# Modulation weights loaded from the POOL queue instead of SP's, transfers of the compressed blocks from ScalarE's

## Chip, cores and metric

The kernel runs on one core of a Trainium2 chip. The metric is the device time of one execution in microseconds (us). The median of three runs of the kernel before is 2730.47 us (2729.22 to 2731.21).

## What is computed

Two transformer blocks run one after the other on one sequence of 256 tokens with 2048 channels, all in float32. The change touches only the start of the first block: the modulation (adaLN), which gives six vectors of 2048 channels from a 2048 x 12288 matrix, and the compressed blocks of one of the four token mixers.

```python
def first_block(x, c, ...):
    c_act = jax.nn.silu(c)
    mod = c_act @ ada_w[l] + ada_b[l]                    # 2048 x 12288
    sh1, sc1, g1, sh2, sc2, g2 = jnp.split(mod, 6, axis=-1)
    h = rmsnorm(x, norm1_g[l]) * (1.0 + sc1[:, None]) + sh1[:, None]
    x = x + g1[:, None] * token_mixer(h, w_in[l], ...)   # four attention mixers
    h = rmsnorm(x, norm2_g[l]) * (1.0 + sc2[:, None]) + sh2[:, None]
    x = x + g2[:, None] * moe_ffn(h, ...)                # 16 experts
    return rmsnorm(x, final_g)
# second_block: a Hyena mixer, whose long filters depend on the weights alone and are
# computed at the start of the kernel; a gating unit; a dense feed-forward layer
```

## The kernel before

The program is unrolled, and a scheduler of the language gives each engine a fixed order of instructions by priorities and estimated times. Float32 products are made of three products of split parts: each chunk of weights, 128 x 1024 values or 512 KB, is loaded (L178) into a ring of five buffers (tag "wraw"), ScalarE rounds it to its high part (L144), VectorE subtracts for the low part (L147), and TensorE multiplies (L156 to L158). There are three buffers for each part.

The first stage has two phases. `phase0` loads the sequence (xT, L491), computes the filters of the second block (`filters`, at low priority: its last layer at L532, with weights loaded at L494 and a decay loaded at L497, its transforms at L549 to L559), and then goes through four blocks of 512 channels. For each block, `ada_steps` computes shift and scale, `norm_mod` makes h of the block, and `feed` multiplies it with the first columns of w_in. The modulation of the next block runs along with the products of this one. `mixers` then computes the other products of w_in and the four attention mixers, and a hook places the rest of the modulation (four more vectors) between them.

Every modulation load is a piece of 256 rows x 512 columns, 512 KB; there are 192 of them, 64 in `phase0`, 16 for each block. They share four buffers (tag "a"). All are issued from SP's queue (L438), the one that loads the ring too, so that all loads of weights stand in one line. Half of the pieces behind `phase0` are multiplied on VectorE (L446, L448), all others on TensorE (L444). At the end of `phase0` the variable `last_ada` holds the last load, and the loads of the next product (columns from 4608) are tied behind it by `tc.issue_after`.

`cmp_blocks` copies keys and values within SBUF to a layout with two tokens on the partitions: eight transfers from POOL's queue (L881, L882), which wait for a copy of ScalarE (L602), and memsets on POOL. `compress` multiplies these blocks after the product with the columns from 4608. POOL has no other work but a few memsets. ScalarE's queue issues small loads, the store of the filters (L571) and the bias tables (L764).

Of the kernel before, what the change touches and what calls it, by code (L numbers as in the profile page):

```python
# [15 lines left out]
PSUM = bass.MemoryType.PSUM  # L16
DRAM = bass.MemoryType.DRAM

P = 128
S = 256  # L20
D = 2048
KD = D // P
# [10 lines left out]
def _constants():  # L33
    """Arrays that depend on the shapes alone."""
    c = {}
# [24 lines left out]
    # compressed blocks [2 x 15] to 16 rows a head, and the head of each row  # L60
# [6 lines left out]
    # The DFT of 512 points of real data: planes of cos at 0..127, cos at 128, 255..129, -sin at both; the sine of 0  # L67
    # makes room for the highest frequency
    turn = 2 * np.pi / 512
# [10 lines left out]
    # the same by even and odd points: cos and -sin at 0..127 for even, for odd, then both at 128  # L80
# [15 lines left out]
def host(inputs):  # L96
    """The arrays of the launch."""
    a = {n: np.asarray(t) for n, t in inputs.items()}
    given = {n: np.ascontiguousarray(a[n]) for n in _NAMES}
    given.update(_layout(a, _constants()))  # L100
    return given


def _rows(*parts):
    """Parts [rows <= 128, columns] side by side, on 128 rows."""
    return np.concatenate([np.pad(p, ((0, P - len(p)), (0, 0))) for p in parts], 1)


def _layout(a, c):
    """Small arrays side by side, vectors by channel, x with its channels first."""  # L110
# [4 lines left out]
    w = {}  # L115
# [16 lines left out]
# columns of p_vec behind the square matrices, by 128 channels  # L132
# [5 lines left out]
class Body:  # L138
# [14 lines left out]
    def mm3(self, ps, a, b, start, stop):  # L153
        """ps (+)= a.T @ b for pairs (hi, lo) of stationary a and moving b."""
# [14 lines left out]
    def rload(self, src, kt, n, tag=None):  # L169
        """The DMA of a chunk of weights into the ring, or into a piece."""  # L170
# [10 lines left out]
    def wload(self, src, kt, width, perm=False):  # L181
        """kt row tiles x width columns of a float32 matrix -> (hi, lo).

        perm: columns of heads 0..7 in the order 0 4 1 5 2 6 3 7."""
# [19 lines left out]
    def gemm(self, w, nk, col0, width, xs, pieces, hook=None, perm=False):  # L204
        """Products of the columns col0.. of w [nk*128, *] with the activations.

        pieces: ("C", c, n): channel-major [n<=128 columns from c, 256 tokens];
                ("T", c, n, tok): token-major [128 tokens of tile tok, n columns from c].
        xs(k): the (hi, lo) channel-major activations of row tile k.
        """  # L210
# [8 lines left out]
    def accumulators(self, pieces):  # L219
        """PSUM of the pieces of a gemm: a bank holds two channel-major ones."""  # L220
# [12 lines left out]
    def feed(self, ps, w, k0, n, nk, col0, width, xs, pieces, perm=False):  # L233
        """The n row tiles from k0 of a gemm."""
        src = w[k0 * P:(k0 + n) * P, col0:col0 + width].rearrange("(k p) n -> p k n", p=P)
        wh, wl = self.wload(src, n, width, perm)
        for ip, p in enumerate(pieces):
            for kk in range(n):
# [4 lines left out]
                if p[0] == "C":  # L243
                    # two accumulators of a bank: the first product of one opens both, the last of the other closes both
# [12 lines left out]
    def sq_acc(self, acc, src, k, scale=1.0):  # L257
        """acc (+)= (src * scale)**2."""
# [8 lines left out]
    def scaled_split(self, hh, hl, k, g):  # L267
        """(hi, lo) of xT * g for row tile k; the factors of the tokens follow behind the products."""
# [12 lines left out]
    def token_ms(self, *parts):  # L281
        """Mean squares + eps of each token, [128 tokens, 2], from parts of the sums of each partition."""
# [10 lines left out]
    def token_rsqrt(self, v, then=None):  # L293
        """v[:, 2:4] = 1/sqrt(v[:, 0:2]), with one Newton step. then: a function whose table to load behind the root."""
# [7 lines left out]
    def spread(self, r):  # L302
        """[128 tokens, 2] -> the same 256 values on every partition."""
# [16 lines left out]
    def run(self):  # L320
# [25 lines left out]
        # pieces of 1024 values a partition: modulation weights, keys and values, then weights and tokens of experts  # L346
# [17 lines left out]
    def phase0(self):  # L364
        nc, tc, i = self.nc, self.tc, self.i
        tc.cur_priority = 10000
        with ExitStack() as c0:
# [3 lines left out]
            # silu(c), one column per row tile, in 32 equal columns each  # L371
# [15 lines left out]
            # Shift and scale by blocks of 512 channels, h of each block, and its products with the first  # L387
            # columns of w_in
# [6 lines left out]
            # the modulation of a block runs along with the products of the block before it  # L395
# [19 lines left out]
    def norm_mod(self, hh, hl, k, rstd, g, sc, sh):  # L415
        """(hi, lo) of row tile k of h = xT * rstd * g * (1 + scale) + shift, channel-major."""
# [10 lines left out]
    def ada_steps(self, seg, b, dve=False):  # L427
        """512 channels of one of the six vectors, in 4 steps of four row tiles: on VectorE, or on TensorE, which
        takes the four at a time, on 32 columns each. The sums come together behind a turn of rows to columns."""
# [4 lines left out]
        for q in range(4):  # L434
            for h in range(2):
                k0 = 4 * q + 2 * h
                raw = self.piece([P, 2, 512], "a")
                self.last_ada = nc.sync.dma_start(raw, w[k0 * P:(k0 + 2) * P, c0:c0 + 512]  # L438
                                                  .rearrange("(k p) n -> p k n", p=P))
# [42 lines left out]
    def filters(self):  # L482
# [21 lines left out]
        # the last layer comes twice, on the two halves of the partitions  # L504
# [18 lines left out]
        for o in range(2):  # L523
            for hf in range(2):
# [27 lines left out]
                # a sum over the even points and one over the odd points give two frequencies  # L552
# [21 lines left out]
    def mixers(self):  # L574
# [9 lines left out]
        bg, last = rest(), self.last_ada  # L584
# [9 lines left out]
        with ExitStack() as c0:  # L594
# [21 lines left out]
            # D  # L616
# [7 lines left out]
            with tc.issue_after(last.ins):  # L624
# [971 lines left out]
```

## Time and profile before

| What | Value |
|---|---|
| Median of three runs | 2730.47 us |
| Span of the profiled execution | 2723.2 us |
| Mean granted clock of TensorE (share of full speed) | 0.988 |
| TensorE busy | 2625.9 us (96%) |
| VectorE, ScalarE busy | 1797.8 us (66%), 1335.5 us (49%) |
| POOL busy | 5.3 us, 18 instructions |
| DMA moved | 640.81 MB, mean 235 GB/s |

The profiled execution's own time is known by its span, from the first to the last instruction. The three runs were timed without a profile; their median is 7.3 us above that span, which is what lies around it. Busy times are those of instructions: matmuls are pipelined, and one that waits inside the pipeline counts as busy. PE is TensorE, PEld its loading of weights, DVE VectorE, ACT ScalarE; "SPq", "ACTq" and "POOL ... DMA_DIRECT2D" are transfers being issued. "L444" is line 444 of the kernel. "[2.39 <-ACT whi L144]" behind an instruction is the time that its engine stood idle before it, and what ended it.

### The profile page before, as it was taken

What the parts mean: (1) busy time and instruction counts of PE and PEld (TensorE: products, weight loads), DVE (VectorE), ACT (ScalarE), POOL (GpSimd) and SP (SyncE); (2) the same over time, 40 slices, a digit from 0 to 9 for tenths busy, and PEclk for the clock granted to TensorE, in tenths of its full rate; (3) what the DMA queues carried; (4) which work ended last, traced back from release to release, by engine and by line L of the source; (5) the groups of instructions that cost most, each with busy time, mean ns of one, the idle gap of its engine ahead of it and who ended that gap; (6) DMA issues with size and microseconds to landing.
All of it is one profiled execution on the core that took longest, in us unless ns stands there. A gap on an engine that the chain in (4) does not pass through costs nothing.

```text
span 2723.2 us, 43658 instructions
## 1 busy us (share of the span) xinstructions
PE 2625.9 (96%) x17355; PEld 2274.9 (84%) x17355; DVE 1797.8 (66%) x2509; ACT 1335.5 (49%) x1774; POOL 5.3 (0%) x18
## 2 busy tenths in 40 slices
PE   6999999998999999999999899999999999999997
PEld 2467888897778776776998899999999999998886
DVE  4547767777888887887777655555655555555444
ACT  2333444546777766676444444444544444443443
POOL 0000000000000000000000000000000000000000
PEclk8999999998999999999999999999999999999999
DMA  8898898983999999996654566666566666666664
GB/s 305 305 308 293 294 320 301 329 294 107 314 323 309 331 322 331 321 338 236 182 158 139 166 183 183 183 185 186 181 184 185 181 184 184 181 185 193 186 188 136
DMA packets 320083, 640.81 MB, mean 235 GB/s; under 512 B 21564, under 2 KB 35420, under 8 KB 319104
## 3 DMA queue, kind: packets, MB, share of 16 engines
q1 hardware_dynamic: 310768, 618.83, 69.7%
q10 hardware_dynamic: 8848, 18.61, 2.0%
q8 instruction: 137, 2.24, 0.3%
q0 software_dynamic: 256, 0.52, 0.1%
q14 instruction: 74, 0.61, 0.1%
HBM read 631.01 MB, written 6.35 MB: 234 GB/s over the span
## 4 chain that ended last, share of the span: by engine, by line
PE 59%; DMA 8%; DVE 5%; ACT 3%; issue 1%; ACTq 1%; DVEq 0%; SPq 0%
PE ps_mm L158 16%; PE ps_mm L157 16%; PE ps_mm L156 16%; DVE wlo L147 4%; DMA wraw<-in_exp_w_down_dram 3%; DMA wraw<-in_exp_w_up_dram 3%; ACT whi L144 2%; DMA wraw<-in_exp_w_gate_dram 1%; PE ps_y L157 1%; PE ps_u L157 1%; PE ps_y L158 1%; PE ps_y L156 1%; PE ps_u L158 1%; PE ps_u L156 1%; PE ps_g L157 1%
## 5 line engine op out<-in xcount | busy, mean ns | idle before, releaser
L147 DVE TENSOR_TENSOR wlo<-wraw,whi 128x1024 fp32r<-128x1024 f32 (+1 forms) x972 | 1165.8, 1205 | 712.2 <-ACT whi L144 701.2
L144 ACT ACTIVATE whi<-wraw 128x1024 fp32r<-128x1024 f32 (+1 forms) x972 | 1011.6, 1044 | 1029.9 <-PE ps_mm L157 550.0
L156 PE MATMUL ps_mm<-hH,whi 128*128 128x256 f32 x3216 | 917.6, 285 | 8.5 <-ACT whi L144 7.1
L158 PE MATMUL ps_mm<-hH,wlo 128*128 128x256 f32 x3216 | 913.9, 285 | 2.8 <-DVE wlo L147 2.8
L157 PE MATMUL ps_mm<-hL,whi 128*128 128x256 f32 x3216 | 912.8, 284 | 0.0
L156 PEld LDWEIGHTS ps_mm<-hH,whi 128*128 128x128 f32 x3216 | 616.3, 192 | 31.7 <-issue 13.8
L158 PEld LDWEIGHTS ps_mm<-hH,wlo 128*128 128x128 f32 x3216 | 615.3, 192 | 17.3 <-DVE wlo L147 8.2
L157 PEld LDWEIGHTS ps_mm<-hL,whi 128*128 128x128 f32 x3216 | 616.4, 192 | 5.0 <-issue 4.6
L157 PE MATMUL ps_mm<-wlo,actH 128*128 128x512 f32 x352 | 139.3, 396 | 0.0
L158 PE MATMUL ps_mm<-whi,actL 128*128 128x512 f32 x352 | 139.1, 395 | 0.0
L156 PE MATMUL ps_mm<-whi,actH 128*128 128x512 f32 x352 | 139.0, 395 | 0.0
L157 PE MATMUL ps_y<-wlo,piece 128*128 128x512 f32 x256 | 106.4, 416 | 8.4 <-DVE wlo L147 7.8
L444 PE MATMUL ps_ada<-piece,cact 128*32 128x512 f32 x512 | 102.2, 637 | 7.3 <-DMA piece<-in_ada_w_dram 6.6
L158 PE MATMUL ps_y<-whi,piece 128*128 128x512 f32 x256 | 101.3, 397 | 0.0
L156 PE MATMUL ps_y<-whi,piece 128*128 128x512 f32 x256 | 92.7, 403 | 2.1 <-ACT piece L144 1.4
L448 DVE SCALAR_TENSOR_TENSOR arow<-piece,cs,arow 128x512 f32<-128x512 f32 x120 | 89.4, 745 | 0.9
L157 PEld LDWEIGHTS ps_mm<-wlo,actH 128*128 128x128 f32 x352 | 66.0, 187 | 16.3 <-DVE wlo L147 0.2
L156 PEld LDWEIGHTS ps_mm<-whi,actH 128*128 128x128 f32 x352 | 66.0, 187 | 16.0
L158 PEld LDWEIGHTS ps_mm<-whi,actL 128*128 128x128 f32 x352 | 66.0, 187 | 15.9
L157 PEld LDWEIGHTS ps_y<-wlo,piece 128*128 128x128 f32 x256 | 48.4, 189 | 34.6 <-DVE wlo L147 24.0
L156 PE MATMUL ps_mm<-mgH,whi 128*128 128x256 f32 x256 | 71.9, 281 | 0.0
L157 PE MATMUL ps_mm<-mgL,whi 128*128 128x256 f32 x256 | 71.9, 281 | 0.0
(446 smaller groups left out, 3486.8 us busy)
## 6 DMA issues: line engine op xcount, KB each, us to landing
wraw<-in_w_in_dram SPq DMA_DIRECT2D x224, 512.0 KB, 4.6
piece<-in_ada_w_dram SPq DMA_DIRECT2D x192, 512.0 KB, 5.0
wraw<-in_w_ffn_in_dram SPq DMA_DIRECT2D x176, 512.0 KB, 4.5
wraw<-in_exp_w_down_dram SPq DMA_DIRECT2D x125, 512.0 KB, 5.8
wraw<-in_exp_w_up_dram SPq DMA_DIRECT2D x124, 512.0 KB, 5.0
wraw<-in_exp_w_gate_dram SPq DMA_DIRECT2D x122, 512.0 KB, 5.0
wraw<-in_w_ffn_out_dram SPq DMA_DIRECT2D x88, 512.0 KB, 3.7
wraw<-in_w_out_dram SPq DMA_DIRECT2D x64, 512.0 KB, 5.1
```

The costliest lines, as they stand in the source:

```text
L144: self.nc.scalar.activation(dst, src, AF.Copy)
L147: self.nc.vector.tensor_tensor(dst, src, h.bitcast(F32), OP.subtract)
L156: mm(ps, a[0], b[0], start=start, stop=False)
L157: mm(ps, a[0], b[1], start=False, stop=False)
L158: mm(ps, a[1], b[0], start=False, stop=stop)
L444: nc.tensor.matmul(ps[m:m + 32], self.cact[:, k], r, start=q == 0, stop=q == 3)
L448: nc.vector.scalar_tensor_tensor(sb, r, self.cs[:, k:k + 1], sb, OP.mult, OP.add)
```

## The change

All modulation pieces are loaded from POOL's queue. The eight transfers of the compressed blocks go from POOL's queue to ScalarE's, and the six memsets in `cmp_blocks` and `nsa` from POOL to VectorE, so that POOL's queue holds modulation loads alone. The tie of the loads for columns 4608 behind the last modulation load is taken out, as it held on SP's queue. The numbers of buffers, the sizes and the arithmetic stay the same. The rest of the diff takes out comments.

```diff
@@ ada_steps
                 raw = self.piece([P, 2, 512], "a")
-                self.last_ada = nc.sync.dma_start(raw, w[k0 * P:(k0 + 2) * P, c0:c0 + 512]
-                                                  .rearrange("(k p) n -> p k n", p=P))
+                nc.gpsimd.dma_start(raw, w[k0 * P:(k0 + 2) * P, c0:c0 + 512]
+                                    .rearrange("(k p) n -> p k n", p=P))
...
@@ mixers
-        bg, last = rest(), self.last_ada
+        bg = rest()
...
-            with tc.issue_after(last.ins):
-                for m, p in enumerate(self.gemm(w, KD, 4608, 512, xs, C4, hook)):
-                    take(kv[:, m], p)
+            for m, p in enumerate(self.gemm(w, KD, 4608, 512, xs, C4, hook)):
+                take(kv[:, m], p)
...
@@ cmp_blocks
-        nc.gpsimd.memset(kk[64:, :, 255:], 0.0)
+        nc.vector.memset(kk[64:, :, 255:], 0.0)
         for h in range(2):
-            nc.gpsimd.dma_start(kk[:64, h], src[h * 64:h * 64 + 64])
-            nc.gpsimd.dma_start(kk[64:, h, :255], src[h * 64:h * 64 + 64, 1:])
+            nc.scalar.dma_start(kk[:64, h], src[h * 64:h * 64 + 64])
+            nc.scalar.dma_start(kk[64:, h, :255], src[h * 64:h * 64 + 64, 1:])
         blk = mp.tile([P, 16, 2, 16], F32, name="blk", tag="s", bufs=3)
-        nc.gpsimd.memset(blk[:, :, :, 15:], 0.0)
+        nc.vector.memset(blk[:, :, :, 15:], 0.0)
...
@@ nsa
-            nc.gpsimd.memset(s, 0.0)
+            nc.vector.memset(s, 0.0)
```

## Rows read from the trace of the kernel before

**Rows 1.** The page: its first line and TensorE's busy time, and the modulation loads in its list of issues (count, KB of each, median us from issue to landing).
```profile
span 2723.2 us, 43658 instructions
PE 2625.9 (96%) x17355; PEld 2274.9 (84%) x17355; DVE 1797.8 (66%) x2509; ACT 1335.5 (49%) x1774; POOL 5.3 (0%) x18
...
piece<-in_ada_w_dram SPq DMA_DIRECT2D x192, 512.0 KB, 5.0
```

**Rows 2.** Busy time by stretch. Columns: the stretch, its length, busy us and instructions of PE, PEld, DVE, ACT and POOL, the granted clock of TensorE, DMA's share, GB/s.
```profile
0.00:53.30 53.30, 30.53 (x104) 7.01 (x104) 23.07 (x52) 12.19 (x16) 0.20 (x4) 0.87 0.86 294
53.30:162.00 108.70, 103.06 (x556) 51.31 (x556) 61.88 (x126) 32.69 (x58) 0.69 (x5) 1.00 0.88 308
162.00:176.00 14.00, 11.65 (x83) 11.34 (x83) 7.16 (x13) 7.54 (x16) 0.00 (x0) 0.88 1.05 394
176.00:565.00 389.00, 382.76 (x2882) 320.01 (x2881) 284.35 (x498) 178.55 (x360) 4.37 (x9) 0.99 0.89 303
```

**Rows 3.** The same view in slices of 4 and 2 us.
```profile
4.00:8.00 4.00, 1.11 (x2) 0.28 (x2) 1.04 (x3) 0.21 (x1) 0.00 (x0) 1.00 1.08 444
...
16.00:20.00 4.00, 3.84 (x16) 0.84 (x14) 4.00 (x1) 1.10 (x1) 0.00 (x0) 1.00 0.88 263
...
28.00:32.00 4.00, 3.21 (x8) 0.66 (x7) 1.24 (x2) 0.00 (x0) 0.00 (x0) 0.50 0.50 145
...
60.00:64.00 4.00, 2.04 (x11) 0.56 (x8) 3.96 (x8) 2.21 (x4) 0.00 (x0) 1.00 1.05 396
...
170.00:172.00 2.00, 2.00 (x19) 2.00 (x18) 1.23 (x1) 1.31 (x3) 0.00 (x0) 1.00 1.03 396
```

**Rows 4.** The timeline of SP's queue from the start: when a run of issues began, how long it took from the first to the last, line, tile and source, number of issues.
```profile
1.65 0.43 SPq L491 DMA_DIRECT2D xT<-in_p_x_dram  x1
2.13 42.19 SPq L438 DMA_DIRECT2D piece<-in_ada_w_dram  x20
44.36 0.46 SPq L178 DMA_DIRECT2D wraw<-in_w_in_dram  x1
44.88 1.26 SPq L494 DMA_DIRECT2D piece<-in_p_w_dram  x2
...
46.88 1.30 SPq L497 DMA_DIRECT2D piece<-in_k_decay_dram  x2
```

**Rows 5.** The timelines of ScalarE, VectorE and TensorE near the first products: start, duration, instruction, idle time before it.
```profile
26.39 0.42 ACT L518 ACTIVATE fh<-fa 128x256 f32<-128x256 f32 x1
...
43.95 0.69 DVE L459 COPY arow<-ps_ada 128x512 f32<-128x512 f32 x1 [9.30 <-PE ps_ada L444]
...
53.30 0.39 PE L156 MATMUL ps_mm<-hH,whi 128*128 128x256 f32 x1 [2.39 <-ACT whi L144]
...
53.97 1.13 PE L532 MATMUL ps_b<-piece,fh 64*128 64x512 f32 x2
```

**Rows 6.** TensorE's groups of instructions by line from 53.3 to 175 us, those of the filters: count, busy us, mean ns of one, idle time before.
```profile
L557 PE MATMUL ps_b<-piece,fdft 128*128 128x512 f32 x32 | 16.8, 623 | 0.2 <-DVE piece L540 0.2
L532 PE MATMUL ps_b<-piece,fh 64*128 64x512 f32 x32 | 13.3, 642 | 0.0
L549 PE MATMUL ps_b<-vec,piece 128*128 128x1 f32 x64 | 8.4, 253 | 1.7 <-DVE piece L545 1.7
L559 PE MATMUL ps_b<-piece,fdft 128*1 128x512 f32 x16 | 8.2, 591 | 0.0
```

**Rows 7.** SP's waits from 44 to 162 us (us in total, times, the longest); the modulation loads of 44 to 160 us (shortest, median and longest issue in ns, first and last start) and the landing of the pieces in that stretch; last, the landing in the stretch from 160 to 570 us.
```profile
SPq L438 <- PE ps_ada L444: 69.6, 31, 7.1
...
L438 SPq DMA_DIRECT2D piece<-in_ada_w_dram x45: 367/368/1016, 43.9 to 153.4; - x45
...
DMA to landing us min/median/max: 3.8/5.3/10.4
...
DMA to landing us min/median/max: 3.5/5.4/7.6
```

**Rows 8.** The timelines of TensorE and of SP's queue near 340 us: two bursts of products of pieces (four records for a piece) and the loads between them.
```profile
339.20 1.92 PE L444 MATMUL ps_ada<-piece,cact 128*32 128x512 f32 x16
348.58 2.20 PE L444 MATMUL ps_ada<-piece,cact 128*32 128x512 f32 x16
...
340.29 2.16 SPq L438 DMA_DIRECT2D piece<-in_ada_w_dram  x4
```

**Rows 9.** Transfers of POOL and of ScalarE: the first four of POOL's eight by tile, and the landing of all eight; ScalarE's store of the bias table (48 KB) by tile, and its landing; an instruction of VectorE that ran while POOL issued; VectorE's products of a piece with a scalar, by tile.
```profile
L881 POOL DMA_DIRECT2D kk<-piece x4: 523/523/656, 176.2 to 179.4; - x4
...
DMA to landing us min/median/max: 5.2/6.0/6.5
...
L479 ACTq DMA_DIRECT2D ebias_d<-ebias x1: 335/335/335, 29.5 to 29.5; - x1
DMA to landing us min/median/max: 1.6/1.6/1.6
...
177.12 2.36 DVE L147 TENSOR_TENSOR wlo<-wraw,whi 128x1024 fp32r<-128x1024 f32 x2 [5.20 <-ACT whi L144]
...
L446 DVE TENSOR_SCALAR arow<-piece,cs x8: 470/478/488, 206.7 to 550.8; 128x512 f32<-128x512 f32 x8
```

**Rows 10.** The timeline of ScalarE where the keys and values to be compressed are copied out.
```profile
175.48 0.66 ACT L602 ACTIVATE piece<-ps_mm 128x256 f32<-128x256 f32 x2 [2.22 <-PE ps_mm L158]
176.02 2.01 ACT L144 ACTIVATE whi<-wraw 128x1024 fp32r<-128x1024 f32 x2
```

## The prediction

> **What bounds the kernel now.** The change touches only the stage before the experts, so I read that stage first. The page says that TensorE is busy for 96% of a span of 2723.2 us [rows 1]; a share over the whole kernel does not say what one stage waits for, so the next view is the busy time by stretch [rows 2]. The reader should see four stretches. From 0 to 53.3 us TensorE is busy for 30.53 us only, at a mean clock of 0.87, while DMA moves 294 GB/s. From 53.3 to 162 us it is busy for 103.06 of 108.70 us. A short end of the phase follows, from 162 to 176 us, and then 176 to 565 us with 382.76 of 389.00 us busy. So behind 176 us there is almost no idle time to win (6.2 us); what can be won lies before it.
>
> Second, is DMA full? In slices of 2 and 4 us [rows 3] the engines move 390 to 444 GB/s when loads of several kinds are under way (4 to 8, 60 to 64, 170 to 172 us), and 263 and 145 GB/s when modulation pieces are the only loads (16 to 20, 28 to 32 us). The share column reads 0.88 at 263 GB/s, so it is no measure of fullness here: what limits is how many loads are in flight. The modulation has four slots (tag "a").
>
> Third, SP's order [rows 4]: behind xT come 20 modulation loads that take until 44.3 us to issue, since each waits for a slot; the first chunk of w_in (44.36), the filters' last layer (44.88) and the decay (46.88) stand behind them. The price is in rows 5: the filters' input is ready at 26.8 us, their first matmul of the last layer comes at 53.97, and the first product of w_in at 53.30, after waiting 2.39 us for the split of a chunk that was not there earlier, while the last sum of its block's modulation was read at 43.95.
>
> Fourth, the recycling of the slots [rows 7]. From 44 to 160 us, 45 modulation loads are issued. Four slots times 109 us over 45 loads is 9.7 us a turn, of which 5.3 us is landing and 4.4 us waiting for TensorE; SP's own waits agree (69.6 us of that stretch for TensorE to free a slot). The pieces are there before TensorE wants them.
>
> **The change, part by part.**
> **1. Start of the first product.** Before the first product the chip must move, by the size of a piece [rows 1] and the shapes of the tiles loaded [rows 4], in KB: 16 modulation pieces of 512, five ring chunks of 512, xT 2048, the last layer 1024, the decay 1024 and some 1.7 MB of small arrays, 16.9 MB in all. Before, the ring's chunks, the last layer and the decay came behind the 16 pieces. At 390 GB/s [rows 3] this takes 43 us, when the first block's modulation is complete now too (DVE reads its sum at 43.95 [rows 5]); at the 294 GB/s of the whole stretch [rows 2] it takes 57 us, 14 us late. I take the first end plus a little, since two queues will be deep at once as at 60 to 64 us: the block is 2 us later, but its chunk is split already, so the product starts at 50 instead of 53.3 us: **-3 us** (bounds -5 to +11).
>
> **2. Filters under the modulation.** Their four groups of matmuls are busy 16.8 + 13.3 + 8.4 + 8.2 = 46.7 us, all behind 53.3 us [rows 6], 11.7 us for each of four quarters. Up to the end of the last layer SP then has 4.35 MB (2.8 MB up to xT, a chunk, the layer); at half of 390 GB/s that is 22 us, so the filters run from about 30 us, and in 20 us some 1.7 quarters are done, 20 us of TensorE work that leaves the stretch from 53.3 to 162. Per turn of the slots (45 loads are 11 turns) that is 1.7 us less waiting: 9.7 becomes 8.0 us, and over the 48 pieces of the other three blocks, 12 turns, 20 us. The filters' chains through VectorE and ScalarE, and the sum at the end of each block, which waits for VectorE, do not shrink; I take half: **-10 us** (bounds 0 to -20). The cover of this part is that the pieces still land in time, which is part 3.
>
> **3. Landing from POOL's queue.** No modulation load from POOL is in the trace. The nearest rows are the eight small transfers that POOL issues now [rows 9]: 64 KB each, 5.2 us at the least from issue to landing, while ScalarE's transfer of 48 KB landed in 1.6 us. So a load from POOL lands between 0 and 3.6 us later than one from SP; below nothing too if leaving SP's line saves it a wait, which the 69.6 us for slots [rows 7] makes small. POOL needs 0.52 us for 64 rows; a piece has 256 runs of 2 KB, so 0.52 to 2.1 us of issue, below the 2.4 us between loads in that stretch. I take 1.8 us, the middle, as the eight small ones came into traffic of 396 GB/s [rows 3] and the 48 KB into 145 [rows 3]. Then a turn is 5.3 + 1.8 + 0.9 us of TensorE's own use (half of the 1.92 us that four pieces take [rows 8]) = 8.0 us: just what part 2 needs, no cost there. From 176 us on the average turn is 4 x 389 / 128 = 12.2 us, which has room. But bursts have none: four pieces go at 339.20, their loads are issued to 342.45, and the next four are used at 348.58 [rows 8]; with 5.4 us of landing [rows 7] the last is 0.7 to 0.9 us early. About five such places in this stage (an estimate, one or two for each attention) cost 1.8 - 0.9 us each: **+4 us** (bounds 0 to +14).
>
> **4. Transfers of the compressed blocks on ScalarE's queue.** Eight issues of 0.34 us, by ScalarE's row [rows 9], 2.7 us in all, come right behind the copy at 175.48 and ahead of the two splits at 176.02 [rows 10]. The next split comes 2.7 us later, and the chunk that is split by then covers some of it, so TensorE stands for 0 to 2.7 us; I take **+1.5 us**. The blocks are ready earlier, but their products come behind the next 512 columns of w_in, so that earns nothing.
>
> **5. The rest.** Six memsets go from POOL to VectorE, and VectorE is busy for 7.16 of the last 14 us of the phase [rows 2]: nothing. The five chunk loads that were tied behind the last modulation load may go earlier; only three chunks can be split ahead, so nothing. Ring loads no longer stand behind modulation loads on SP; all of TensorE's idle time behind 176 us is 6.2 us, and I count none of it.
>
> **Sum:** -3 - 10 + 4 + 1.5 = -7.5 us. The profiled execution spans 2723.2 us and the median of the three runs is 2730.47, 7.3 us more around the span; nothing there changes. **2723 us.** This kernel's measurement tells about 0.2%, 5.5 us, from no change.
>
> **A rule against the change.** Rows 3 show 444 GB/s with several kinds of load under way and 263 with one. The Trainium skill (DMA: Bandwidth & Descriptors, section Issuing engines are not separate DMA queues) says that loads of all queues run on the same 16 engines and that spreading them saves only issue time. By it parts 1 and 2 would be nothing; that is the first rival. The trace agrees that the engines are shared but not that they are full.
>
> A second rule is that of the Trainium skill, SBUF — State Buffer, section Who interferes with whom: POOL cannot write descriptors while VectorE runs a copy or a product with a scalar from SBUF in its faster mode. No run here shows a modulation load under such an instruction. POOL's issues kept their 0.52 us while VectorE ran L147 from 177.12 us [rows 9], and the instructions of the other sort in this stage (L446) are 8 of 0.478 us, 4 us in all [rows 9]. So by that rule the sum would be 2723 to 2727.
>
> **Rivals.**
> *No change, the modulation sets the pace.* The filters move forward, but the stretch keeps its 9.7 us a turn, because the chain of four pieces, a sum and a product is serial. Then -3 + 1.5: 2729 us. For it: DMA and TensorE both look 88 to 95% used in rows 2. Against it: 4.4 us of each turn is waiting for TensorE. Chance 0.25.
> *Late landings, slower.* At 3.6 us the turn is 5.3 + 3.6 + 0.9 = 9.8 us, so part 2 earns nothing, the bursts cost 5 x 2.7 = 13.5 us, and with -3 and +1.5 the sum is +12: 2742 us. Place: the loads of L438 and the TensorE waits behind them at L444. Each us of landing past 1.8 costs 12 + 5 us until part 2 is used up, so it turns into a loss from about 2.3 us. For it: every POOL transfer in the trace took 5.2 us or more. Chance 0.28, with up to 2750 if issue is also 2.1 us.
> *A larger gain.* POOL's loads land as SP's do and all 20 us of part 2 come: -3 - 20 + 1.5, 2709 us. Chance 0.12.
>
> **How the numbers follow.** The forecast, 2715 to 2725 us, has 0.35; the larger gain 0.12; so faster by over 0.2% 0.47, within it 0.25, slower 0.28. Range: 2708 to 2743, which leaves out the far ends of both outer cases; the likeliest case's own is 2715 to 2726.
>
> **What would show it.** Right: the first last-layer matmul of the filters (L532) near 30 us, the first product of w_in at about 50, and the copy behind the last first-phase product, now at 175.48, 8 to 13 us earlier, with DMA above 330 GB/s before 53 us. Part 3 is read from the landing of the modulation loads: 7 us is the forecast, 9 the loss. Part 4 is a gap of TensorE near that copy. Wrong if L444 waits for its loads more than 10 us behind 53 us, if the first block is complete behind 50 us, or if the stages from the experts on differ by more than 2 us.

## The result, and the profile after

The change makes the kernel slower: 2747.74 us (median of four runs, 2743.10 to 2751.74) against 2730.84 us for the kernel before (four runs), a ratio of 1.0053, 95% interval 1.0034 to 1.0073. That is 17 us; 2723 us was forecast. Measured again among the experiments, the ratio was 1.0065 (1.0045 to 1.0085).

The page of the kernel after first: its span, the busy time of the engines, the queue of POOL (packets, MB, share of the 16 engines), and the groups of the modulation's loads and products (busy us, mean ns, idle time before them and what ended most of it).

```profile
span 2741.4 us, 43685 instructions
PE 2635.8 (96%) x17355; PEld 2269.1 (83%) x17355; DVE 1796.7 (66%) x2515; ACT 1333.9 (49%) x1774; POOL 139.1 (5%) x196
...
q0 software_dynamic: 27648, 100.68, 10.3%
...
L438 POOL DMA_DIRECT2D piece<-in_ada_w_dram x192 | 138.9, 724 | 446.9 <-PE ps_ada L444 233.3
L444 PE MATMUL ps_ada<-piece,cact 128*32 128x512 f32 x512 | 119.7, 626 | 27.2 <-DMA piece<-in_ada_w_dram 25.9
```

POOL now issues all 192 loads, 0.72 us each, and has time to spare: it stood idle for 447 us before them, for slots that TensorE (233 us) or VectorE still held. The line to notice is the last. TensorE waited 25.9 us for modulation pieces to land, and its modulation products were busy for 119.7 us. The line numbers of the kernel after are one lower from the middle of `mixers` on.

The stretches of [rows 2] in the kernel after, with the same columns:

```profile
0.00:53.30 53.30, 30.89 (x104) 6.96 (x104) 28.89 (x62) 15.72 (x22) 15.40 (x25) 0.94 1.00 381
53.30:162.00 108.70, 105.47 (x544) 48.44 (x540) 53.94 (x117) 29.50 (x53) 35.10 (x50) 1.00 0.90 307
162.00:176.00 14.00, 13.78 (x95) 11.41 (x96) 7.63 (x12) 5.27 (x9) 1.13 (x2) 1.00 0.60 192
176.00:565.00 389.00, 368.35 (x2724) 302.56 (x2723) 270.60 (x475) 170.69 (x353) 81.68 (x113) 0.98 0.84 289
```

Up to 176 us TensorE is busy for 150.1 us, 4.9 us more than the 145.2 of [rows 2]; DMA moves 381 GB/s at the start instead of 294. Behind 176 us TensorE is busy for 14.4 us less in the same time, so that is where work falls behind. The end of the stage confirms it: the experts' first product starts at 659.11 us, after 638.98 before, and what follows it takes 2082.3 and 2084.2 us, the same.

The start, in the timelines of SP's queue and of POOL (start, time from the first issue of a run to the last, line, tile, source, number of issues):

```profile
1.65 0.43 SPq L491 DMA_DIRECT2D xT<-in_p_x_dram  x1
2.13 0.43 SPq L178 DMA_DIRECT2D wraw<-in_w_in_dram  x1
2.60 1.15 SPq L494 DMA_DIRECT2D piece<-in_p_w_dram  x2
...
4.34 2.88 SPq L497 DMA_DIRECT2D piece<-in_k_decay_dram  x2
13.09 27.61 SPq L178 DMA_DIRECT2D wraw<-in_w_in_dram  x7
```

```profile
1.29 3.00 POOL L438 DMA_DIRECT2D piece<-in_ada_w_dram  x4 [0.82 <-POOLq L1583]
15.42 0.72 POOL L438 DMA_DIRECT2D piece<-in_ada_w_dram  x1 [11.14 <-PE ps_ada L444]
```

SP's loads are free of the modulation, as the change says: the filters' last layer is asked for at 2.60 us instead of 44.88 [rows 4]. But it then shares the start with the first four pieces, and POOL's fifth load has to wait for one of their slots until 15.42 us. The 16 loads of the first block are issued by 39.4 us.

Last, TensorE's waits for pieces (us in total, times, the longest) in the kernel after ahead of 280 us and behind it, and in the kernel before behind 270 us:

```profile
PE ps_ada L444 <- DMA piece<-in_ada_w_dram: 19.4, 16, 5.4
PE ps_ada L456 <- DVE arow L448: 8.8, 1, 8.8
```

```profile
PE ps_ada L444 <- DMA piece<-in_ada_w_dram: 6.5, 8, 1.3
```

```profile
PE ps_ada L444 <- DMA piece<-in_ada_w_dram: 0.2, 1, 0.2
```

The line with 8.8 us is a single wait, the longest of TensorE in this stage. The sum of a vector that VectorE multiplies (L456) stands there on TensorE; the last products of it (L448) stand behind a split on VectorE (L147), that one behind ScalarE's part of the same split (L144), and ScalarE waits for a chunk of the ring to land. From the timelines of ScalarE, VectorE and TensorE (start, duration, instruction, idle time before it):

```profile
218.60 1.06 ACT L144 ACTIVATE whi<-wraw 128x1024 fp32r<-128x1024 f32 x1 [10.31 <-DMA wraw<-in_w_in_dram]
...
219.69 1.22 DVE L147 TENSOR_TENSOR wlo<-wraw,whi 128x1024 fp32r<-128x1024 f32 x1 [8.32 <-ACT whi L144]
220.83 2.32 DVE L448 SCALAR_TENSOR_TENSOR arow<-piece,cs,arow 128x512 f32<-128x512 f32 x3
...
223.29 0.99 PE L456 MATMUL ps_ada<-vec,arow 128*128 128x1 f32 x4 [8.77 <-DVE arow L448]
```

Why that chunk landed so late was not followed up.

### The profile page after: what moved, and what is told of

Its sections match the earlier page's. It is cut to its first block, busy times and chain, and to the rows that moved or that the text cites. A ratio compares the mean times of both kernels' runs of the same rounds, so it can differ in the third digit from the quotient of the medians.

```text
span 2741.4 us, 43685 instructions
## 1 busy us (share of the span) xinstructions
PE 2635.8 (96%) x17355; PEld 2269.1 (83%) x17355; DVE 1796.7 (66%) x2515; ACT 1333.9 (49%) x1774; POOL 139.1 (5%) x196
## 4 chain that ended last, share of the span: by engine, by line
PE 58%; DMA 9%; DVE 5%; ACT 2%; issue 1%; ACTq 1%; DVEq 0%; SPq 0%
PE ps_mm L158 16%; PE ps_mm L157 16%; PE ps_mm L156 16%; DMA wraw<-in_exp_w_down_dram 4%; DVE wlo L147 3%; DMA wraw<-in_exp_w_up_dram 3%; ACT whi L144 2%; DMA wraw<-in_exp_w_gate_dram 1%; PE ps_u L157 1%; PE ps_u L158 1%; PE ps_y L157 1%; PE ps_u L156 1%; PE ps_y L158 1%; PE ps_y L156 1%; PE ps_g L156 1%
## 5 line engine op out<-in xcount | busy, mean ns | idle before, releaser
L147 DVE TENSOR_TENSOR wlo<-wraw,whi 128x1024 fp32r<-128x1024 f32 (+1 forms) x972 | 1165.0, 1205 | 711.3 <-ACT whi L144 701.6
L144 ACT ACTIVATE whi<-wraw 128x1024 fp32r<-128x1024 f32 (+1 forms) x972 | 1011.6, 1044 | 1104.3 <-PE ps_mm L157 609.0
L438 POOL DMA_DIRECT2D piece<-in_ada_w_dram x192 | 138.9, 724 | 446.9 <-PE ps_ada L444 233.3
L444 PE MATMUL ps_ada<-piece,cact 128*32 128x512 f32 x512 | 119.7, 626 | 27.2 <-DMA piece<-in_ada_w_dram 25.9
L448 DVE SCALAR_TENSOR_TENSOR arow<-piece,cs,arow 128x512 f32<-128x512 f32 x120 | 89.5, 745 | 3.2 <-DMA piece<-in_ada_w_dram 2.1
L444 PEld LDWEIGHTS ps_ada<-piece,cact 128*32 128x32 f32 x512 | 17.8, 110 | 75.3 <-DMA piece<-in_ada_w_dram 44.2
L158 PEld LDWEIGHTS ps_mm<-whi,actL 128*128 128x128 f32 x352 | 66.0, 187 | 15.9
```

The costliest lines, as they stand in the source:

```text
L144: self.nc.scalar.activation(dst, src, AF.Copy)
L147: self.nc.vector.tensor_tensor(dst, src, h.bitcast(F32), OP.subtract)
L158: mm(ps, a[1], b[0], start=False, stop=stop)
L438: nc.gpsimd.dma_start(raw, w[k0 * P:(k0 + 2) * P, c0:c0 + 512] .rearrange("(k p) n -> p k n", p=P))
L444: nc.tensor.matmul(ps[m:m + 32], self.cact[:, k], r, start=q == 0, stop=q == 3)
L448: nc.vector.scalar_tensor_tensor(sb, r, self.cs[:, k:k + 1], sb, OP.mult, OP.add)
```

## The experiments

Times are compared with the kernel before, run on the same chip between them. On these chips single runs of one kernel spread more than at first (the kernel before from 2721 to 2746 us), so ratios and their intervals decide, and a profile's span is only one draw.

**Parts and halves: e1 to e3, e5 to e8.** Each takes the kernel before and moves some of the loads. The edits, with kk's transfers and memsets moved or not (e2, e5, e7 and e8 also take the tie out, as the change does; e1, e3 and e6 keep it):

```diff
-                self.last_ada = nc.sync.dma_start(raw, ...
+                self.last_ada = (nc.gpsimd if seg < 2 else nc.sync).dma_start(raw, ...   # e2, e5: phase 0
+                self.last_ada = (nc.sync if seg < 2 else nc.gpsimd).dma_start(raw, ...   # e3, e6: mixers
+                self.last_ada = nc.gpsimd.dma_start(raw, ...                             # e7, e8: all
-            nc.gpsimd.dma_start(kk[:64, h], src[h * 64:h * 64 + 64])
+            nc.scalar.dma_start(kk[:64, h], src[h * 64:h * 64 + 64])                     # e1, e2, e3, e8
```

> The kernel before with one part of the change alone: the eight transfers of kk go out on ScalarE's queue and the three memsets run on VectorE; the modulation stays on SP's queue with its tie. Theory A (the loss comes from the modulation loads of phase 0 on POOL's queue, which change the order of TensorE's products) and theory B (it comes from late landings in the mixers) both say no change, 2729 to 2733 us. Theory C (eight issues of 0.6 us ahead of the splits on ScalarE hold the compressed blocks up) says 2735 to 2740 us.

> The change with POOL's queue only for the two vectors of phase 0 (64 of 192 loads); the 128 loads of the mixers go out on SP's queue as before. Theory A: all of the loss arises in phase 0 and at its end, so about as slow as the changed kernel, 2742 to 2750 us, with the last filter product near 180 us instead of 162. Theory B (late landings of the mixers' loads behind 176 us): the loss goes, 2722 to 2732 us.

> The mirror image: the 64 loads of phase 0 on SP's queue, the 128 loads of the mixers on POOL's queue, with kk on ScalarE's. Theory A: the order of phase 0 is that of the kernel before, the last filter product near 162 us, and the time is 2726 to 2734 us. Theory B: the loss stays, 2740 to 2750 us, with TensorE waiting for the modulation's loads behind 176 us.

> POOL's queue for the 64 modulation loads of phase 0 and nothing else: the 128 loads of the mixers stay on SP's queue, and kk stays on POOL's queue as in the kernel before. The sum theory (each part has its own price whatever the others do: kk on ScalarE's queue 1.0036 from the first experiment, phase 0 on POOL's queue 1.0015 less 1.0036, so some 6 us gained) says 0.9979 of the kernel before, 2724 to 2732 us. The order theory (kk costs only where its transfers stand behind the 1 MB bias transfer in ScalarE's queue, which the late filters undo) says that phase 0 on POOL's queue costs by itself: 1.001 to 1.003.

> POOL's queue for the 128 modulation loads of the mixers and nothing else: phase 0 on SP's queue with its order, kk on POOL's queue. The sum theory (1.0076 with kk on ScalarE's queue, less 1.0036 for kk) says 1.003 to 1.005. The order theory says the same here, for the order of ScalarE's queue is that of the first experiment in both. A third, that the mixers' loads on POOL's queue cost only together with the kk wait (both fall into the stretch from 185 to 230 us), says 0.998 to 1.001.

> The change without its second half: all 192 modulation loads on POOL's queue, kk left on POOL's queue among them (73 loads stand ahead of it), memsets on POOL. The sum theory (the changed kernel 1.0053 less 1.0036 for kk) says 1.001 to 1.003. The order theory (kk costs nothing in the changed kernel, its transfers landed in 2.0 us there) says 1.004 to 1.007, the changed kernel's own ratio. If kk is held up on POOL's queue behind loads that wait for a slot, it is over 1.007.

> The changed kernel as it is, beside the parts on the same chip. Both theories say 1.0034 to 1.0073, the interval measured first.

| Modulation loads on POOL's queue | kk on POOL's queue | kk on ScalarE's queue |
|---|---|---|
| none | 1 (the kernel before) | e1: 1.0036 (1.0019 to 1.0054) |
| phase 0, 64 loads | e5: 0.9988 (0.9974 to 1.0002) | e2: 1.0015 (1.0001 to 1.0030) |
| mixers, 128 loads | e6: 1.0054 (1.0035 to 1.0073) | e3: 1.0076 (1.0056 to 1.0096) |
| all 192 | e7: 1.0051 (1.0033 to 1.0069) | e8, the change: 1.0065 (1.0045 to 1.0085) |

The first theory (A: the loss arises in phase 0, whose order on TensorE changes) fell with e3, and half with e2, which came out between A and B; that kk costs nothing, as A and B had it, fell with e1. The medians of e1 (2746 us) and e3 (2753 us) lie above every range named for them. e6 is just above what the sum and the order theory allowed, e7 in the range of the order theory and above that of the sum theory. The left column says it plainly: the mixers' loads on POOL's queue cost 0.54%, 15 us, with nothing else changed, and phase 0's (with the tie taken out) gain 0.12%, some 3 us. The two halves add up within the intervals (0.9988 + 1.0054 - 1 = 1.0042, measured 1.0051). kk has no single price: 0.36% in e1, 0.22 to 0.27% beside one half of the loads, 0.14% in the changed kernel, less than the intervals tell.

The 8.8 us wait of the changed kernel (L456) is there again in its second profile (9.2 us) and in e7 (6.6), and shorter in e2 (4.2). In e5, e6 and e3 all waits of that line behind 160 us come to 1.0 us or less. What e6 shows instead is waits for pieces, 12.2 us from 160 to 640 us.

**Broken steps: e4.** A modulation step takes two pieces and runs four products side by side, each on 32 columns of TensorE. The timeline of the changed kernel, phase 0 (four records are one piece):

```profile
100.16 1.05 PE L444 MATMUL ps_ada<-piece,cact 128*32 128x512 f32 x4
101.14 0.38 PE L157 MATMUL ps_mm<-hL,whi 128*128 128x256 f32 x1
...
102.05 1.05 PE L444 MATMUL ps_ada<-piece,cact 128*32 128x512 f32 x4
```

One piece takes 1.05 us by itself; a whole step took 1.06 us elsewhere in this timeline. In the changed kernel steps stand in halves more often, and from 53 to 180 us the modulation's products are busy for 49.2 us (200 records) where they took 35.7 (178) before. So e4 puts the halves together:

```diff
-                    if not dve:
-                        m = 32 * (2 * h + j)
-                        nc.tensor.matmul(ps[m:m + 32], self.cact[:, k], r, start=q == 0, stop=q == 3)
+                if not dve:
+                    raws.append(raw)
+                    if h:          # behind both loads: products 2, 3, 0, 1, the last three tied behind the first
+                        ...
```

> The changed kernel with one difference: the four products of a modulation step (two loads, 32 columns of TensorE each) are written behind both loads, and three of them are tied behind the one that uses the second load, so that a step's products stand together. In the changed kernel's order on TensorE a step is broken up often: 98 groups for 64 steps, here 76. A half step took 1.05 us in the trace of the changed kernel and a whole step 1.06. Theory A1 (broken steps are the loss): 22 groups by 1 us less, 2722 to 2730 us. Theory A2 (the late filters and the stall behind them are the loss; the last filters stand later still in this order): 2740 to 2750 us, no gain. If both have a share: 2732 to 2738 us.

It came out at 1.0120 (1.0099 to 1.0141), slower than the change. TensorE's waits in e4 up to 700 us, in a kernel whose products stand in L447:

```profile
PE ps_ada L447 <- DMA piece<-in_ada_w_dram: 57.6, 24, 7.7
```

The theory's price was wrong by its sign. A half step fills TensorE while the second piece is still under way; held until both are there, it becomes a wait (57.6 us instead of 25.9). So joining the halves by force makes late pieces dearer. The halves themselves are not made by pieces that come late in the run: TensorE's order is fixed beforehand. The two profiled executions of the kernel before have its 17355 records in the same order but for two of them, and those of the change too; e6 has 929 at another place than the kernel before, though only the queue of the loads differs. Most edits here change that order as well, and no run holds it fixed.

**Slots: e9, e10, e13, e14.** If pieces land later, a fifth slot should cover it. In e9 and e10 the room comes from the ring:

```diff
-    PIECES = {"a": 4, "k": 3, "v": 2, "m": 4}
+    PIECES = {"a": 5, "k": 3, "v": 2, "m": 4}
...
-        self.nraw, self.nsplit = 5, 3
+        self.nraw, self.nsplit = 4, 3
```

The small filter buffer that the first expectation names kept its two copies in both.

> The changed kernel with five slots for the modulation's pieces instead of four; the ring has four slots instead of five to make room (and one small filter buffer one copy instead of two). Theory L (a piece from POOL's queue lands about 1 us later, 6.3 instead of 5.1 us in the mixers, and four slots do not cover that: TensorE waits 6.5 us for pieces there and its pieces come apart): the fifth slot covers it, the wait for pieces behind 280 us falls under 2 us, the stretch of the mixers that took 379 us falls to 368 to 372 us, and the time to that of the same slots with SP's queue, within 0.2%. Theory O (not the slots: the queue itself, its traffic beside the ring's): the wait stays at 5 us or more and the time 0.4% or more above that of the next kernel.

> The control: the kernel before with five slots for pieces and four in the ring. Both theories: TensorE hardly waited for pieces in the mixers of the kernel before (0.2 us behind 270 us), so the fifth slot brings nothing, and the ring's lost slot costs 0 to 8 us: 0.999 to 1.003.

The ring of four cost far more than allowed for: 1.0372 (e9) and 1.0277 (e10), and e10's expectation failed. e9 is 0.95% above e10, where theory L allowed 0.2% and theory O named 0.4% or more: by the totals this pair speaks against theory L. In the profiles e9 is 9.5 us longer, 8.1 of them ahead of the experts' first product; the rest of the 21 us between the medians was not followed up. The stretch of the mixers can be read by itself. From the 700th record of the ring's products (near 280 us) to the experts' first product it took 370.3 us in e9 and 369.1 in e10, where the change took 378.6 and 379.5 in its two profiles. TensorE waited 4.4 us for pieces in e9, not under 2. With four slots this stretch took 376.7 to 379.5 us in the five profiles with the mixers on POOL's queue (the change twice, e3, e6, e7), and with SP's queue 366.2 to 369.4 in six (the kernel before, e1, e2, e5, e15, e18) but 375.1 and 375.7 in two others (e11, e12). The granted clock of TensorE in the stretch goes with it: 0.98 in the six, 0.97 in the two, and 0.98 in all with POOL's queue but e3 (378.8 us at 0.97). So one profile proves little, but with four slots the two queues stand 7 us or more apart at 0.98 (3 us at 0.97). In e13 and e14 the ring is whole, and the room comes from buffers of the norms and one of the filters:

```diff
-        sq = self.tmp.tile([P, S], F32, name="sq", tag="sq", bufs=4)
+        sq = self.tmp.tile([P, S], F32, name="sq", tag="sq", bufs=1)
...
-        t = self.tmp.tile([P, S], F32, name="hn", tag="hn", bufs=3)
+        t = self.tmp.tile([P, S], F32, name="hn", tag="hn", bufs=2)
...
-            a = p0.tile([P, S], F32, name="fa", tag="fa", bufs=2)[:m]
+            a = p0.tile([P, S], F32, name="fa", tag="fa", bufs=1)[:m]
```

> The sixth kernel (mixers' modulation loads on POOL's queue, nothing else) with five slots for pieces and the ring whole; the room comes from small buffers of the norms and one of the filters (one square instead of four, two normed tiles instead of three). With four slots it was 1.0054 of the kernel before. Theory L (late landing against four slots): within 0.2% of the same buffers with SP's queue (the next kernel). Theory O (the queue or its traffic): 0.4 to 0.7% above the next kernel, as with four slots.

> The control: the kernel before, on SP's queue throughout, with five slots and the same small buffers. Both theories: the fifth slot brings little, since TensorE hardly waited for pieces in the mixers; the smaller norm buffers may cost some us: 0.998 to 1.003 of the kernel before.

e13 is at 1.0000 (0.9985 to 1.0014), e14 at 0.9993 (0.9979 to 1.0007): 0.07% apart, within the 0.2% that theory L allowed, where four slots were 0.54% apart. (The stretch took 372.0 us in e13 at a clock of 0.98 and 376.3 in e14 at 0.97; the totals decide.) The landing of the modulation loads (shortest, median, longest) and TensorE's wait for them, all from 280 to 600 us; e14 lists no such wait. First the kernel before (SP's queue, four slots):

```profile
L438 SPq DMA_DIRECT2D piece<-in_ada_w_dram x93: 367/368/1571, 279.7 to 564.8; - x93
...
DMA to landing us min/median/max: 3.5/5.1/7.6
```

then e6 (POOL's queue, four slots):

```profile
L438 POOL DMA_DIRECT2D piece<-in_ada_w_dram x96: 722/722/731, 282.5 to 585.4; - x96
...
DMA to landing us min/median/max: 3.9/6.1/9.9
```

```profile
PE ps_ada L444 <- DMA piece<-in_ada_w_dram: 5.7, 5, 1.6
```

and e13 (POOL's queue, five slots):

```profile
DMA to landing us min/median/max: 4.0/6.5/11.6
```

```profile
PE ps_ada L444 <- DMA piece<-in_ada_w_dram: 3.3, 4, 1.8
```

Over the whole of the mixers, from 160 to 640 us, the same wait in e6 and then in e13:

```profile
PE ps_ada L444 <- DMA piece<-in_ada_w_dram: 12.2, 8, 5.7
...
PE ps_ada L444 <- DMA piece<-in_ada_w_dram: 9.8, 8, 3.6
```

The pieces of e13 land as late as those of e6, and in the totals the loss is gone: with five slots the queue or its traffic costs nothing that can be told. That the fifth slot does it by covering one microsecond of landing is not shown. TensorE still waits 9.8 us for pieces in e13, and 8.7 in e17 where the change has 9.3; what makes up for them was not found, and the order on TensorE differs too.

**kk ahead of the bias: e15.** In e1 the 1 MB transfer of the bias stands ahead of kk on ScalarE's queue; in the changed kernel, whose filters end later, it stands behind (line L763). The timeline of ScalarE's queue in e1:

```profile
183.00 0.38 ACTq L764 DMA_DIRECT2D bias<-ebias_d  x1
187.21 0.51 ACTq L881 DMA_DIRECT2D kk<-piece  x1
187.75 0.61 ACTq L882 DMA_DIRECT2D kk<-piece  x1
188.41 0.61 ACTq L881 DMA_DIRECT2D kk<-piece  x1
193.87 0.47 ACTq L882 DMA_DIRECT2D kk<-piece  x1
```

Three issues go out, and the fourth stands for 4.9 us; the splits of the ring's chunks stand behind it on ScalarE. VectorE, whose sums of kk are ahead of its own half of the splits, waited 15.9 us. e15 ties the bias behind kk:

```diff
-        bias = self.load_bias(3)
+        with self.tc.issue_after(self.last_kk.ins):
+            bias = self.load_bias(3)
```

> The first kernel (kk on ScalarE's queue alone, 1.0036) with the 1 MB bias transfer tied behind the last of the eight kk transfers on the same queue, as it happens to stand in the changed kernel. Theory K (kk's transfers waited in the queue behind the bias: the fourth was issued 4.9 us after the third, VectorE waited 10.5 us for the first two): VectorE's wait for kk falls under 5 us and the time to 0.999 to 1.001. Theory C (eight issues of 0.6 us on ScalarE hold the splits up): no change, 1.003 to 1.005.

VectorE's waits for kk in e1, and under it in e15 (170 to 235 us):

```profile
DVE blk L889 <- DMA kk<-piece: 15.9, 3, 10.5
```

```profile
DVE blk L889 <- DMA kk<-piece: 4.1, 3, 2.7
```

The wait falls as theory K said, and kk lands 2.1 us after its issue instead of 6.2. The time falls to 1.0017 (0.9998 to 1.0037), between the two expectations; the intervals of e1 and e15 overlap. That the place behind the bias is what made kk wait is shown by the rows; that it is the whole of 0.36% is not. TensorE's order changes with it: 1214 records of e1 stand at another place than in the kernel before, 24 of e15.

**The start: e11.** As e5, but the first 16 loads go on SP's queue ahead of the rest (`nc.gpsimd if seg < 2 and b else nc.sync`).

> The fifth kernel (POOL's queue in phase 0 alone) with the first 16 loads, which the first products wait for, back on SP's queue ahead of everything else: POOL's queue takes the 48 loads of the other three blocks. The forecast's part one had the first product at 50 us; it came at 57 in every kernel with POOL's queue in phase 0. If SP's loads for the filters and the ring, which start at once beside POOL's, take the first pieces' share of the DMA engines (early contention): the first product falls back to 50 to 54 us and the time is 3 to 6 us below the fifth kernel's, 0.996 to 0.998 of the kernel before. If not: 0.998 to 1.000 as the fifth kernel.

The first product came at 53.98 us, as early contention says, instead of 57.25 in e5. The time didn't follow: 1.0042 (1.0029 to 1.0056). From the 257th to the 385th record of the ring's products it took 39.3 us, where e5 took 27.0; the filters' last layer still stood in that stretch, 2.0 us of it, beside 8.2 us of modulation products where e5 had 3.0. An earlier start moved work to the end of the phase, and more is not known.

**The kernel before once more: e12.**

> The kernel before as it is, for a second profile. In the profiles of the two kernels that kept phase 0 of the kernel before, the granted clock fell to 0.5 to 0.6 in the stretch from 53 to 82 us and the 193rd product of w_in came at 160 to 166 us; in the first profile of the kernel before it was 1.00 there and the product came at 155 us. If the dip belongs to the kernel before as well, it shows here or the times spread by about 10 us between executions; if it belongs to those kernels alone, the 193rd product is at 155 us again.

It took 2740.47 us, and the 193rd product came at 158.51 us, between the two expectations. TensorE in slices from 53 us in the first profile of the kernel before (columns as in [rows 2]), and in e12:

```profile
53.00:62.00 9.00, 8.32 (x40) 4.27 (x40) 4.93 (x9) 1.63 (x4) 0.00 (x0) 1.00 1.05 391
62.00:72.00 10.00, 8.41 (x42) 4.18 (x42) 6.04 (x12) 3.57 (x7) 0.00 (x0) 1.00 0.69 233
```

```profile
53.00:62.00 9.00, 7.92 (x35) 5.20 (x34) 3.54 (x7) 1.04 (x2) 0.00 (x0) 0.73 0.94 348
62.00:72.00 10.00, 8.07 (x32) 3.26 (x32) 4.45 (x9) 2.81 (x6) 0.00 (x0) 0.83 0.48 156
```

The dip of the clock belongs to the kernel before too. The same stretch was at 0.53 to 0.74 in e1, e3, e6 and e15, which keep its phase 0, and at 1.00 in every four-slot profile with all of phase 0 on POOL's queue (the change twice, e2, e4, e5, e7, e18).

**The version that the runs point to: e16, e18, and the whole change with five slots, e17.** e16 is e5 and e17 the change, both with the slots and buffers of e13; e18 is e5 again.

> The fifth kernel (POOL's queue for phase 0 alone, 0.9988 of the kernel before) with five slots and the small buffers of the two kernels above. If the late landing against four slots also costs in phase 0 (TensorE waited 18.0 us for pieces ahead of 278 us there): 0.993 to 0.998. If those waits belong to the start, where the pieces come one after another whatever the slots: 0.998 to 1.002.

> The changed kernel with five slots for pieces, the ring whole, and the small buffers of e13 and e14. If the mixers' late landing against four slots is the changed kernel's loss: its ratio (1.0053, again 1.0065) falls to that of phase 0 on POOL's queue with kk on ScalarE's, 1.000 to 1.003. If there is another cause in the queue: 1.005 or more.

> The fifth kernel again: POOL's queue for the 64 loads of phase 0 alone, four slots. If it is faster than the kernel before by something that can be told: 0.996 to 0.999. If phase 0 gives back at its end what it gains at its start: 0.999 to 1.002.

e18 is at 0.9987 (0.9973 to 1.0001), as e5 was: each interval just reaches 1, two equal results together speak for some 3 us. It is the best version here: faster than the change, and a little faster than the kernel before. e16 is at 1.0024 (1.0008 to 1.0039) and e17 at 1.0037 (1.0024 to 1.0050). With five slots, then, the step from phase 0 alone to the whole change is 0.13%; with four it was 0.66% (1.0053 less 0.9987) or more. That agrees with theory L in the totals; in the rows it is the long wait of L456 that is gone (0.3 us in e17), while the waits for pieces stay. And e17 missed its range: the whole change with five slots is still 0.44% above the kernel before with five (e14), as a fifth slot made phase 0 on POOL's queue slower by 0.36% (e16 against e5). Why stays open: TensorE waited less for pieces there, 13.7 us ahead of 280 us instead of 18.0, and the rows name no other wait that carries 10 us. The first product comes later (59.89 us, 57.25 in e5), and from 53 to 62 us the granted clock is 0.77 where e5 has 1.00.

## Why the prediction was wrong

**The step that failed is part 3, by its size.** The mechanism was named, late landing as a rival with its place at L438 and L444, and the mixers' loads by themselves show it: from 160 to 640 us TensorE waits 12.2 us for pieces in e6 and 0.2 in the kernel before. Its own sign of being wrong, more than 10 us of such waits behind 53 us, came with 12.1 in the change. The price was wrong. Part 3 took 1.8 us of later landing, let 0.9 us of it pass for nothing and got 4 us behind 176 us. Measured, the landing in the mixers is about 1 us later (6.1 us in e6, 6.3 in the change, 5.1 before), for which the same working gives 0.5 us (five times 1.0 less 0.9); the mixers' loads cost 15.

The slack of 0.7 to 0.9 us had been read at one place, near 340 us, and was taken for all. The estimate of about five bursts was near the truth behind 280 us, where e6 has five waits, 5.7 us in all. The other 6.5 us of its 12.2 lie ahead, 5.7 of them in one wait at 173 us, where the mixers' first four loads land; the forecast looked for bursts in the middle of the stage and not at its start. The rest of the 15 us is not laid out. In the changed kernel the waits for pieces behind 160 us come to 9.3 us, and the wait of L456 adds 8.8, for which the forecast had no term. A fifth slot takes the mixers' loss out of the totals (e13); by which of these terms, the runs leave open. The average turn of 12.2 us was no comfort, since the waits come where pieces are used together.

**Part 1** (-3 us, first product at 50) failed. The product came at 56.82 us, inside the bounds on the other side. The forecast took the early bandwidth as free; 381 GB/s is nearly the 390 that it assumed, but SP's loads took their part first: POOL could issue four pieces and then nothing until 15.42 us. **Part 2** (-10 us) came as 3 us for parts 1 and 2 together. The filters' last layer began at 45.06 us, not at 30, and TensorE's idle time from 53 to 180 us did shrink (8.3 to 3.5 us), but the modulation's products took 13.5 us longer there, for 22 records more; at the old 0.20 us a record that is 9 us too much. **Part 4** (+1.5 us) is not contradicted in the changed kernel (e8 less e7 is 0.14%, within both intervals), by luck: in e1, where the bias stands ahead of kk on ScalarE's queue, the move cost 10 us. The forecast counted kk's own issues and never looked at what else stood in that queue. **Part 5** was not measured by itself; the tie alone and the memsets alone were not tried.

**The baseline** was one good draw. The sum was made against a span of 2723.2 us, and the 7.3 us to the median were put down to what lies around the span. In the profiles that have both, 1.7 to 2.0 us lie around it. The rest belongs to that one execution, in which the clock did not dip behind 53 us.

**The rules cited.** The first rival rested on all queues using the same engines, as the Trainium skill has it (DMA: Bandwidth & Descriptors, section Issuing engines are not separate DMA queues); by that rule parts 1 and 2 are nothing. The measurement is close to it, 0.12 to 0.13%; the loss of the whole change is not in that rule. The Trainium skill (SBUF — State Buffer, section Who interferes with whom) let POOL be held up by VectorE. No such hold-up shows: the 192 loads took 722 ns at the least to issue and 838 at the most.

## What to carry to other kernels

A queue of its own frees the queue that the loads leave, but the loads keep their slots. Ask what the landing will be on the new queue, how many pieces are used together where the consumer is full, and look for the tightest of those places, the start of a stage among them, before one of them is taken for all. A slot more can take the loss away, as for the mixers here, and can cost elsewhere, as in phase 0. Where a scheduler fixes the order, compare the orders too: moving loads to another queue changed it here. Before small transfers are moved to another engine's queue, read everything that already stands there: a large transfer ahead of them costs more than their issues. And profile the baseline twice before reading one span against a median.

## What was not expected of the hardware

From 53 to 62 us TensorE's granted clock was 1.00 in one profile of the kernel before and 0.73 in another, 0.53 in e1: all, about half and one part in sixteen of that time at 2.4 GHz, the rest at 1.2 (worked out from the two levels). TensorE had been busy for 8.7 to 8.8 of the 13 us ahead in all three, and for 11.8 and 12.3 in the change and in e5, where the clock from 53 to 62 us was 1.00. With five slots and phase 0 on POOL's queue it was 0.77 to 0.83 (e9, e16, e17), and there phase 0 gained nothing (e16). So phase 0 on POOL's queue may owe its 3 us to the clock in this stretch and not to any transfer; no run separates the two.

Slots of the ring are dear: with four instead of five (and one more for pieces) the kernel before took 76 us longer (2.77% of 2733), four to five times what the mixers' loads on POOL's queue cost.
